# A feed-forward block sum in two passes, squares tile by tile, and single PSUM banks from the third pair of units on: one edit to a three-layer kernel

## The chip, the cores and the metric

The kernel runs on one core of a Trainium2 chip. The engines of that core are TensorE (PE), VectorE (DVE), ScalarE (ACT), GpSimd (POOL) and SyncE (SP, which here only issues transfers); data lie in SBUF (128 partitions) and matmul results in PSUM. The metric is the device time of one execution in microseconds (us), as a median over runs.

## The reference

Three residual layers over x of 1024 rows by 1024 columns, all fp32. Only the parts that the change touches, cut from the reference:

```python
fn = rms_norm(h, norm_ffn[l])
g = fn @ ffn_w_gate[l]                                  # 1024 x 2816
g_pad = jnp.pad(g, ((0, 0), (CONV_W - 1, 0), (0, 0)))
g_conv = ffn_conv_b[l] + sum(cw[i] * g_pad[:, i:i + s] for i in range(CONV_W))   # 3 taps
h = h + (jax.nn.silu(g_conv) * (fn @ ffn_w_up[l])) @ ffn_w_down[l]
...
return x + jnp.concatenate([y_a, y_b], axis=-1) @ w_out   # end of the second ("even") layer
```

Ahead of this stand a mixing stage (gated linear attention, "gla", and latent attention, "mla") and a cross attention ("xa"); behind it a state-space layer with a convolution branch ("even", whose end is `conf` in the code) and a differential attention ("odd"). Each adds a projection to the residual h, and rms_norm needs the row sums of squares of h.

## The kernel before, in words

**Numbers.** Every fp32 operand of a matmul is held as two parts, hi (rounded) and lo (the rest), and a product is three matmuls hi·hi, hi·lo, lo·hi (`mm3`, L258 to 265). `split` (L205) makes the parts of a PSUM tile: hi on ACT (L211), lo on VectorE (L212).

**Stages** in the profiled execution, in us from its start: gla and mla to about 640, xa to 759.5, the up projection of the feed-forward (`ffn_up`, L401) from 759.5 to 1226, the down projection (`ffn_down`, L492) to 1478, the even layer to 2187, its end `conf` to 2385, odd to 3091.

**Order.** The Tile framework plans each engine's queue ahead of time, from a priority that grows as the program is written, and from readiness. `later(n)` (L1261) shifts that priority by n for what is written inside it and sets it back at its end; AHEAD is 30. Each engine then works its queue in order. DMA transfers are issued from the queues of SP, of POOL and of ACT, and an issue stands in its engine's queue like any instruction.

**Memory.** `slot(tag)` takes the next buffer of a tagged set in turn; a buffer is free once its last readers are done. PSUM has four single banks of 512 columns (`pa`) and two pairs of banks of 1024 columns (`pb`), handed out by `psum` (L90).

**Residual tiles.** h is eight tiles of 128 x 1024. `load_h` (L94) takes eight buffers and loads tile t into the t-th: in gla (L834, from x), in the down projection (L507, issued from ACT's queue) and in conf (L1533, from `hs`). In conf, the third buffer of the eight lies on `zb`, from which ACT writes the SSD result to `ysp`; conf loads `ysp` back as `c` (L1525) behind the h loads, and casts it on ACT (L1527). `out_proj` (L295) multiplies and adds the result into h (`add_h`, L290); with `stats` it makes, after each fourth tile, the row statistics of four tiles (`row_stats`, L215: four Squares on ACT with a sum, L219, then the reciprocal root).

**Up projection.** The rows of h are two groups of four tiles, the columns two halves, so the product of 1024 x 1024 by 1024 x 256 is a 2 x 2 block product, done with seven block products in place of eight. There are 22 such units: 11 groups of 256 columns, each for the gate weight and then the up weight. A block product is 12 matmuls of 128 x 512 (`prod`). The weight blocks A11, A22, A12 and their sums S1 to S4 are made by `ffn_w` (L314): hi by ACT (L326), lo by VectorE or POOL (L327), sums by POOL (L332, L333, L334, L337). The input blocks B11, B21, B22 and sums T1 to T4 are made once, by `ffn_x` (L344), in two passes over the two row groups. Pass 0 (written inside `later(-AHEAD)`) scales rows, transposes (L359), splits B11 and B21 with `split`, and keeps a third, unrounded copy of each in `rows` (`xt`, ACT L382). Then `between` (L428) issues the two first products A11·B11 (`first`, L421, result copied to `p1`) and A12·B21 of units 0 and 1; the latter two stay in two single banks, `p2`, until their unit reads them. Pass 1 makes for each quarter k of the columns t1 (L387), t2 (L388), the split of B22, t3 and t4 on POOL (L390, L391), and hi and lo of T2, T3, T1 (lo on VectorE, L366) and T4 (lo on POOL, L366). Then the units run: S2·T2, A12·B21, S3·T3, S1·T1, A22·T4, S4·B22, each result added from PSUM by VectorE (`total` L454, `part` L448); a gate unit then does its three-tap convolution (L477, two taps for each of two blocks on VectorE), an up unit multiplies into it on POOL (L450) and stores the block to `yf` from SP's queue (L482). The pool `fg` (L1978) holds four `tmp` buffers for the sums.

**Down projection.** `yr` is loaded from `yf` on SP's queue (L501), cast on ACT (L503), and multiplied; the first transfer is behind the last stores in SP's queue.

## Time and profile before

| | us |
|---|---|
| median of 3 runs | 3098.76 |
| lowest and highest | 3096.89, 3098.79 |
| the profiled execution's own time | 3093.24 |
| its span, first to last instruction | 3091.2 |
| mean granted clock of TensorE in it | 0.980 of full |

Times in the profile are in us from the start of the span. Busy time of an engine is time in which it executes; what stands in brackets behind an instruction in a timeline is the time for which the engine sat idle before it, and what released it. `out<-in` names the tiles an instruction writes and reads. PEclk is the TensorE clock that was granted, as a share of full speed, which is 2.4 GHz; the lower of its two levels is 1.2 GHz.

### The profile page before, as it was taken

Reading aid. Unit: us, or ns where it says so; the run is one execution under the profiler, and the core shown is the slowest. Engines: PE = TensorE matmul, PEld = TensorE weight load, DVE = VectorE, ACT = ScalarE, POOL = GpSimd, SP = SyncE. Lnnn points to the kernel's source line nnn. Section 1 sums busy time; section 2 is a strip of 40 time slices with the busy share of each in tenths; the row PEclk is TensorE's granted clock in tenths of the full one; section 3 lists DMA queues with packets and bytes.
Section 4 is the critical chain, followed back from the end, with each engine's and each line's share of the span. In section 5 each row is a group of like instructions: output and inputs, shape, how many; then the busy total and the mean of one; then the engine's idle time right before and its main releaser. Section 6 shows DMA issues by size and latency. Waiting matters only on the chain.

```text
span 3091.2 us, 39184 instructions
## 1 busy us (share of the span) xinstructions
PE 2907.2 (94%) x14470; PEld 2364.7 (76%) x14470; DVE 2062.9 (67%) x3296; ACT 1196.4 (39%) x2264; POOL 1014.5 (33%) x917
## 2 busy tenths in 40 slices
PE   8999899898799999999998989999999999999998
PEld 7777676677588887788877878787777888878776
DVE  4225889865755555443798979787698454178786
ACT  5421666634433333221432322323234332155654
POOL 2112610122555554321125151524331231121444
PEclk9999999899899999999999999999999999999999
DMA  3012100212122223421311211122522446244531
GB/s 120 28 48 66 35 1 8 69 42 75 48 82 82 85 86 117 166 96 44 99 48 55 62 48 48 59 59 68 211 75 96 121 143 186 78 139 143 167 93 65
DMA packets 179380, 259.93 MB, mean 84 GB/s; under 512 B 16606, under 2 KB 107254, under 8 KB 179190
## 3 DMA queue, kind: packets, MB, share of 16 engines
q1 hardware_dynamic: 157813, 219.69, 22.4%
q10 hardware_dynamic: 16768, 20.98, 2.1%
q0 software_dynamic: 4608, 16.78, 1.4%
q8 instruction: 114, 1.87, 0.2%
q14 instruction: 77, 0.62, 0.1%
HBM read 191.33 MB, written 66.06 MB: 83 GB/s over the span
## 4 chain that ended last, share of the span: by engine, by line
PE 66%; DVE 15%; issue 5%; POOL 4%; ACT 3%; DMA 3%; SPq 0%; POOLq 0%; ACTq 0%; DVEq 0%
PE pa_t L263 16%; PE pa_t L264 16%; PE pa_t L265 15%; PE pb_t L265 3%; PE pb_t L264 3%; PE pb_t L263 3%; DVE acc_t L1311 3%; PE pa_t L941 2%; PE pb_t L1036 1%; PE pa_t L1055 1%; DVE wl_t L202 1%; PE pb_t L1750 1%; PE pb_t L1751 1%; ACT wh_t L197 1%; DVE h_t L292 1%
## 5 line engine op out<-in xcount | busy, mean ns | idle before, releaser
L202 POOL TENSOR_TENSOR wl_t<-wr_t,wh_t 128x349 fp32r<-128x349 f32 (+3 forms) x199 | 239.0, 1207 | 976.0 <-ACT wh_t L197 942.2
L263 PE MATMUL pa_t<-wh_t,x_t 128*128 128x512 f32 (+3 forms) x1024 | 374.3, 366 | 2.6 <-DVE xl_t L212 0.8
L264 PE MATMUL pa_t<-wl_t,x_t 128*128 128x512 f32 (+3 forms) x1024 | 371.3, 363 | 0.3 <-DVE wl_t L202 0.3
L1311 DVE SCALAR_TENSOR_TENSOR acc_t<-u_t,c,acc_t 128x1024 f32<-128x1024 f32 x240 | 339.4, 1416 | 2.9
L197 ACT CAST wh_t<-wr_t 128x1024 fp32r<-128x1024 f32 (+2 forms) x199 | 175.5, 890 | 354.2 <-PE pb_t L264 138.3
L290 DVE TENSOR_TENSOR h_t<-h_t,pa_t 128x512 f32<-128x512 f32 x256 | 173.1, 684 | 175.3 <-PE pa_t L265 171.8
L202 DVE TENSOR_TENSOR wl_t<-wr_t,wh_t 128x675 fp32r<-128x675 f32 (+2 forms) x173 | 170.9, 991 | 169.1 <-ACT wh_t L197 168.6
L263 PE MATMUL pb_t<-x_t,wh_t 128*128 128x512 f32 x608 | 244.3, 402 | 3.7 <-ACT wh_t L197 2.9
L265 PE MATMUL pb_t<-x_t,wl_t 128*128 128x512 f32 x608 | 242.2, 399 | 1.0 <-DVE wl_t L202 1.0
L264 PE MATMUL pb_t<-x_t,wh_t 128*128 128x512 f32 x576 | 231.0, 401 | 0.0
L265 PE MATMUL pa_t<-wh_t,x_t 128*128 128x512 f32 (+3 forms) x640 | 221.4, 346 | 0.0
L263 PEld LDWEIGHTS pa_t<-wh_t,x_t 128*128 128x128 f32 x1024 | 192.3, 188 | 33.6 <-ACT wh_t L197 1.8
L264 PEld LDWEIGHTS pa_t<-wl_t,x_t 128*128 128x128 f32 x1024 | 192.5, 188 | 30.9 <-DVE wl_t L202 2.0
L265 PE MATMUL pa_t<-wh_t,xl_t 128*128 128x512 f32 x512 | 200.4, 392 | 3.0 <-POOL xl_t L1848 2.1
L326 ACT CAST wh_t<-wr_t 128x512 fp32r<-128x512 f32 x154 | 92.1, 620 | 243.0 <-POOL wr_t L334 129.3
L263 PE MATMUL pa_t<-x_t,wh_t 128*128 128x512 f32 x400 | 163.9, 410 | 2.8 <-ACT xt_t L382 2.1
L265 PE MATMUL pa_t<-x_t,wl_t 128*128 128x512 f32 x400 | 158.8, 397 | 0.0
L327 DVE TENSOR_TENSOR wl_t<-wr_t,wh_t 128x512 fp32r<-128x512 f32 x110 | 97.7, 907 | 91.0 <-ACT wh_t L326 91.0
L263 PE MATMUL pa_t<-xh_t,wh_t 128*128 128x512 f32 x352 | 138.9, 395 | 5.3 <-DVE tmp_t L454 4.8
L263 PEld LDWEIGHTS pb_t<-x_t,wh_t 128*128 128x128 f32 x608 | 115.5, 190 | 30.8 <-ACT wh_t L197 3.9
L264 PE MATMUL pa_t<-xt_t,wh_t 128*128 128x512 f32 x352 | 138.2, 392 | 0.4 <-DVE xt_t L366 0.4
L265 PE MATMUL pa_t<-xh_t,wl_t 128*128 128x512 f32 x352 | 137.8, 392 | 0.0
(558 smaller groups left out, 7477.9 us busy)
## 6 DMA issues: line engine op xcount, KB each, us to landing
wr_t<-in_a_w_in SPq DMA_DIRECT2D x46, 512.0 KB
wr_t<-in_c_w_in SPq DMA_DIRECT2D x26, 512.0 KB
wr_t<-in_ffn_w_gate SPq DMA_DIRECT2D x22, 512.0 KB
wr_t<-in_ffn_w_up SPq DMA_DIRECT2D x22, 512.0 KB
yf<-o_t SPq DMA_DIRECT2D x22, 512.0 KB
wr_t<-in_ffn_w_down SPq DMA_DIRECT2D x44, 256.0 KB
yr_t<-yf SPq DMA_DIRECT2D x22, 512.0 KB
h_t<-in_x SPq DMA_DIRECT2D x16, 512.0 KB
```

Of the source, the lines that this page charges most:

```text
L197: nc.scalar.copy(hi, raw)
L202: e.tensor_tensor(*[x[:, c] for x in f], op=ALU.subtract)
L263: mm(out, lh, rh, start=st, stop=False)
L264: mm(out, lh, rl, start=False, stop=False)
L265: mm(out, ll, rh, start=False, stop=en)
L290: self.nc.vector.tensor_tensor(h[t][:, c], h[t][:, c], ps, op=ALU.add)
L292: self.nc.vector.scalar_tensor_tensor(h[t][:, c], ps, rstd[:, t:t + 1], h[t][:, c], op0=ALU.mult, op1=ALU.add)
L326: nc.scalar.copy(hi, src)
L327: eng.tensor_tensor(lo, src, hi.bitcast(F32), op=ALU.subtract)
L941: self.nc.tensor.transpose(pt[:, i * 256 + q * P:i * 256 + (q + 1) * P], w[t0 + q][:, (b0 + i) * P:(b0 + i + 1) * P], self.ident)
L1036: mm(sp[:, c0:c0 + wd], qT[:96, hd, t * P:(t + 1) * P], kT[:96, hd, c0:c0 + wd], start=True, stop=c0 + wd < n)
L1311: nc.vector.scalar_tensor_tensor(acc, u[:, k:k + S], cw31(k, c), acc, op0=ALU.mult, op1=ALU.add)
```

## The change

`load_h` takes its eight buffers rotated by half: tiles 0 to 3 lie in the last four, tiles 4 to 7 in the first four. `out_proj` with `stats` writes the Square of each tile right behind that tile's adds, and the reciprocal root behind the fourth. In pass 0 of `ffn_x`, B11 gets hi on ACT, its unrounded copy on VectorE from PSUM, and lo on POOL from that copy; B21 gets hi and the copy on ACT and lo on VectorE. `between` is called inside `later`, so that the priority is set back behind it. Pass 1 is split in two loops with the new `third` between them: the first makes t1, t2 (now in buffers of h that are no longer used), B22 and T2 with lo on POOL; `third` issues S4·B22 of units 0 and 1; the second makes t3 (now on VectorE), t4, and hi and lo of T3, T1, T4. A pair of banks of `pb`, halved by `two`, holds `p2` and the third product `p3` of each of units 0 and 1, and later S1·T1 and A22·T4 of unit 1; from the third unit on all products use single banks, as before. The last unit's two stores go out on POOL's queue, and `fg` has seven `tmp` buffers.

```diff
--- before.py
+++ after.py
@@ -93,6 +93,7 @@
 
     def load_h(self, src, eng=None):
         h = [self.slot("h", [P, D]) for _ in range(NT)]
+        h = h[NT // 2:] + h[:NT // 2]
         for t in range(NT):
             (eng or self.nc.sync).dma_start(out=h[t], in_=src[t * P:(t + 1) * P, :])
         return h
@@ -306,8 +307,13 @@
                     self.nc.gpsimd.tensor_tensor(h[t][:, c], h[t][:, c], d, op=ALU.add)
                 else:
                     self.add_h(h, t, c, ps, rstd)
-            if stats is not None and t % 4 == 3:
-                stats[t - 3] = self.row_stats(h[t - 3:t + 1])
+            if stats is not None:
+                if t % 4 == 0:
+                    self.ss = self.stat(4)
+                self.nc.scalar.activation(self.psum("pb"), h[t], AF.Square, accum_out=self.ss[:, t % 4:t % 4 + 1])
+                if t % 4 == 3:
+                    stats[t - 3] = self.stat(4)
+                    self.rsqrt(stats[t - 3], self.ss, D, EPS, 4, self.stat)
 
 
 
@@ -341,7 +347,7 @@
         return out
 
 
-    def ffn_x(self, h, st, hf, between):
+    def ffn_x(self, h, st, hf, between, third):
         nc = self.nc
         X = {n: [[x[:, i] for i in range(2)] for x in (self.slot(tag, [P, 2, 512], F32R) for _ in range(4))]
              for n, tag in (("B11", "x"), ("B21", "x"), ("B22", "xz"))}
@@ -373,28 +379,40 @@
                         nc.scalar.activation(t, t, AF.Copy, scale=st[g0][:, j:j + 1])
                     else:
                         v.tensor_scalar(t, t, st[g0][:, j:j + 1], None, op0=ALU.mult)
+                tt, g = [], nc.gpsimd
                 for k in range(4):
                     c1, c2 = self.col("norm_ffn", k), self.col("norm_ffn", k + 4)
                     p1, p2 = turn(g0, k), turn(g0, k + 4)
                     if i == 0:
-                        for n, p, c, r in (("B11", p1, c1, rows[k][0]), ("B21", p2, c2, rows[k][1])):
-                            self.split(*X[n][k], p, c)
-                            nc.scalar.activation(r, p, AF.Copy, scale=c)
+                        r1, r2 = rows[k]
+                        for (hi, lo), p, c, r in ((X["B11"][k], p1, c1, r1), (X["B21"][k], p2, c2, r2)):
+                            nc.scalar.activation(hi, p, AF.Copy, scale=c)
+                            if r is r1:
+                                v.tensor_scalar(r, p, c, None, op0=ALU.mult)
+                                g.tensor_tensor(lo, r, hi.bitcast(F32), op=ALU.subtract)
+                            else:
+                                v.scalar_tensor_tensor(lo, p, c, hi.bitcast(F32), op0=ALU.mult, op1=ALU.subtract)
+                                nc.scalar.activation(r, p, AF.Copy, scale=c)
                         continue
-                    ta, tb = (self.slot("wr", [P, 2, 512]) for _ in range(2))
-                    t1, t2, t3, t4 = ta[:, 0], ta[:, 1], tb[:, 0], tb[:, 1]
-                    b11, b21 = rows[k]
-                    v.scalar_tensor_tensor(t1, p1, c1, b11, op0=ALU.mult, op1=ALU.subtract)
+                    t12 = self.slot("h", [P, 2, 512])
+                    t1, t2 = t12[:, 0], t12[:, 1]
+                    v.scalar_tensor_tensor(t1, p1, c1, rows[k][0], op0=ALU.mult, op1=ALU.subtract)
                     v.scalar_tensor_tensor(t2, p2, c2, t1, op0=ALU.mult, op1=ALU.subtract)
                     self.split(*X["B22"][k], p2, c2)
-                    nc.gpsimd.tensor_tensor(t3, t2, b11, op=ALU.subtract)
-                    nc.gpsimd.tensor_tensor(t4, t2, b21, op=ALU.subtract)
-                    halves("T2", k, t2, v)
+                    halves("T2", k, t2, g)
+                    tt.append((t1, t2))
+                if i == 0:
+                    between(X)
+                    continue
+                third(X)
+                for k, (t1, t2) in enumerate(tt):
+                    t34 = self.slot("wr", [P, 2, 512])
+                    t3, t4 = t34[:, 0], t34[:, 1]
+                    v.tensor_tensor(t3, t2, rows[k][0], op=ALU.subtract)
+                    g.tensor_tensor(t4, t2, rows[k][1], op=ALU.subtract)
                     halves("T3", k, t3, v)
                     halves("T1", k, t1, v)
-                    halves("T4", k, t4, nc.gpsimd)
-            if i == 0:
-                between(X)
+                    halves("T4", k, t4, g)
         return X
 
 
@@ -412,8 +430,8 @@
                 self.wd = self.down_w(0)
 
 
-        def prod(w, x):
-            ps = self.psum()
+        def prod(w, x, ps=None):
+            ps = self.psum() if ps is None else ps
             for k in range(4):
                 self.mm3(ps, [(w[0][:, k], w[1][:, k])], [x[k]], k == 0, k == 3)
             return ps
@@ -429,10 +447,20 @@
             for i in range(2):
                 first(i, X)
             for i in range(2):
-                p2[i] = prod(ws[i]["A12"], X["B21"])
-
-        p2 = {}
-        X = self.ffn_x(h, st, hf, between)
+                p2[i], p3[i] = two()
+                prod(ws[i]["A12"], X["B21"], p2[i])
+
+        def third(X):
+            for i in range(2):
+                prod(ws[i]["S4"], X["B22"], p3[i])
+
+
+        def two():
+            ps = self.psum("pb")
+            return ps[:, 0:512], ps[:, 512:1024]
+
+        p2, p3 = {}, {}
+        X = self.ffn_x(h, st, hf, between, third)
         more()
         gt = {}
         for i, (kind, g) in enumerate(units):
@@ -462,11 +490,12 @@
             if i:
                 load(i + 1)
             u3 = total(u2, prod(w["S3"], X["T3"]))
-            p5 = prod(w["S1"], X["T1"])
+            p5, p4 = two() if i == 1 else (None, None)
+            p5 = prod(w["S1"], X["T1"], p5)
             part(1, hb, u3, p5)
             u4 = total(u2, p5)
-            part(1, ha, u3, prod(w["A22"], X["T4"]), ALU.subtract)
-            part(0, hb, u4, prod(w["S4"], X["B22"]))
+            part(1, ha, u3, prod(w["A22"], X["T4"], p4), ALU.subtract)
+            part(0, hb, u4, p3[i] if i < 2 else prod(w["S4"], X["B22"]))
             if gate:
                 gt[g] = []
                 for j in (0, 1):
@@ -479,7 +508,7 @@
                     gt[g].append(o)
             else:
                 for j in (1, 0):
-                    nc.sync.dma_start(out=yf[2 * g + j], in_=O[j])
+                    (nc.gpsimd if i == len(units) - 1 else nc.sync).dma_start(out=yf[2 * g + j], in_=O[j])
 
 
     def down_w(self, f0):
@@ -1975,7 +2004,7 @@
                 with K.pool("xf", x=8, xh=16, xt=16, xz=4), ExitStack() as fs:
                     def more():
                         hctx.close()
-                        fs.enter_context(K.open(K.pool("fg", o=2, tmp=4, g=2)))
+                        fs.enter_context(K.open(K.pool("fg", o=2, tmp=7, g=2)))
                     K.ffn_up(h, st, hf, yf, cw, more)
                 hctx = K.open(K.pool("h1b", "right", h=8))
                 with K.pool("fd", yr=2, ya=8, yb=8):
```

## Rows read from the trace of the kernel before

**Rows 1.** The page: busy time, share of the span and instructions of each engine.
```profile
PE 2907.2 (94%) x14470; PEld 2364.7 (76%) x14470; DVE 2062.9 (67%) x3296; ACT 1196.4 (39%) x2264; POOL 1014.5 (33%) x917
```

**Rows 2.** Stretches: length, busy PE, PEld, DVE, ACT, POOL (instructions), clock, DMA share, GB/s.
```profile
761.00:778.00 17.00, 4.66 (x20) 2.98 (x20) 13.09 (x26) 11.40 (x22) 8.37 (x7) 0.66 0.43 137
778.00:792.00 14.00, 13.85 (x52) 11.26 (x53) 5.96 (x8) 8.35 (x15) 6.43 (x5) 0.81 0.05 18
792.00:816.00 24.00, 13.27 (x55) 9.30 (x53) 22.20 (x25) 12.09 (x21) 16.32 (x13) 0.72 0.08 23
...
830.00:845.00 15.00, 9.95 (x36) 7.81 (x37) 13.33 (x14) 7.82 (x9) 7.18 (x6) 0.89 0.23 71
845.00:1214.00 369.00, 369.00 (x1629) 305.66 (x1628) 215.01 (x271) 131.27 (x195) 206.50 (x156) 1.00 0.25 83
1226.00:1247.00 21.00, 13.51 (x43) 9.02 (x43) 3.88 (x4) 4.80 (x5) 6.84 (x5) 0.84 0.92 329
2190.00:2215.00 25.00, 21.15 (x90) 16.26 (x89) 14.29 (x28) 5.87 (x7) 1.93 (x2) 1.00 0.87 335
2215.00:2255.00 40.00, 36.22 (x157) 28.75 (x156) 40.00 (x42) 14.13 (x14) 26.44 (x9) 1.00 0.44 169
```

**Rows 3.** Waits of PE, 760 to 830: total us, times, longest.
```profile
PE pa_t L359 <- DVE wr_t L387: 10.0, 4, 4.5
PE pa_t L359 <- ACT xt_t L382: 9.0, 3, 6.0
```

**Rows 4.** Timeline of PE, 838 to 846: start, us, instruction, idle before and releaser.
```profile
838.07 0.80 PE L263 MATMUL pa_t<-xh_t,wh_t 128*128 128x512 f32 x1 [4.76 <-DVE tmp_t L454]
...
845.22 0.39 PE L263 MATMUL pa_t<-x_t,wh_t 128*128 128x512 f32 x1
```

**Rows 5.** Timeline of DVE, 829 to 846.
```profile
831.54 5.87 DVE L477 SCALAR_TENSOR_TENSOR o_t<-g_t,c,o_t 128x1023 f32<-128x1023 f32 x4
```

**Rows 6.** Lines 366 and 387, 755 to 830: duration in ns min/median/max, starts.
```profile
L366 DVE TENSOR_TENSOR xt_t<-wr_t,xh_t x12: 678/1722/1783, 795.3 to 816.0; 128x512 fp32r<-128x512 f32 x12
...
L366 POOL TENSOR_TENSOR xt_t<-wr_t,xh_t x4: 1540/1550/1581, 797.2 to 815.6; 128x512 fp32r<-128x512 f32 x4
...
L387 DVE SCALAR_TENSOR_TENSOR wr_t<-pa_t,c,xt_t x4: 734/743/751, 792.3 to 806.0; 128x512 f32<-128x512 f32 x4
```

**Rows 7.** Timelines of ACT and of POOL in the first pass.
```profile
772.10 2.18 ACT L326 CAST wh_t<-wr_t 128x512 fp32r<-128x512 f32 x4 [3.75 <-POOL wr_t L334]
774.18 0.68 ACT L382 ACTIVATE xt_t<-pa_t,c 128x512 f32<-128x512 f32 x1
...
770.80 1.26 POOL L334 TENSOR_TENSOR wr_t<-wr_t 128x512 f32<-128x512 f32 x1
```

**Rows 8.** Timeline of ACT at the end of the down projection.
```profile
1461.66 1.03 ACT L219 ACTIVATE pb_t<-h_t 128x1024 f32<-128x1024 f32 x1 [1.57 <-DVE h_t L290]
```

**Rows 9.** Timelines of SP and of PE at the start of the down projection.
```profile
1226.46 0.42 SPq L501 DMA_DIRECT2D yr_t<-yf  x1
1228.80 0.32 SPq L482 DMA_DIRECT2D yf<-o_t  x1
1229.16 0.43 SPq L501 DMA_DIRECT2D yr_t<-yf  x1
...
1232.00 0.79 PE L263 MATMUL pa_t<-wh_t,ya_t 128*128 128x512 f32 x1 [5.82 <-ACT ya_t L503]
```

**Rows 10.** Start of conf: SP's timeline, SP's waits, and what line 1527 waited for.
```profile
2197.13 3.37 SPq L97 DMA_DIRECT2D h_t<-hs  x6
...
SPq L97 <- DMA ysp<-zb_t: 7.0, 1, 7.0
...
  DMA c_t<-ysp: 15.8, 2
```

**Rows 11.** The last h load of gla on SP, and tile 3's add on DVE.
```profile
264.81 0.33 SPq L97 DMA_DIRECT2D h_t<-in_x  x1
...
272.19 0.69 DVE L290 TENSOR_TENSOR h_t<-h_t,pa_t 128x512 f32<-128x512 f32 x1 [2.15 <-PE pa_t L265]
```

## The prediction

> **What bounds the kernel now.** I read the busy times of the page first: TensorE is busy for 2907.2 of 3091.2 us, 94% [rows 1], so an edit pays only where TensorE waits, or crawls at its lower clock, inside the stretches that the diff touches. A table by stretch comes next [rows 2]. From 845 to 1214 us, the steady part of the up projection, TensorE is busy for all 369.00 us at clock 1.00: 1629 matmuls, 0.2265 us each, and nothing that frees another engine is worth anything there. The waste lies in five places. At the entry (761 to 778) TensorE is busy for 4.66 of 17 us at 0.66 of full clock; in the second pass (792 to 816) for 13.27 of 24 at 0.72; in the first pair of units (830 to 845) for 9.95 of 15 at 0.89; where the up projection hands over to the down projection (1226 to 1247) for 13.51 of 21 at 0.84; at the start of conf (2190 to 2215) for 21.15 of 25. The last three views say who is late. TensorE's waits between 760 and 830 name the scaled copy `xt` made on ACT (9.0 us, first pass) and VectorE's subtraction L387 (10.0 us in four waits, second pass) [rows 3]. The timeline shows one more stop, 4.76 us up to 838.07, released by VectorE's `total` L454 [rows 4]: VectorE had spent 5.87 us from 831.54 on four conv taps [rows 5] while the four single banks, one of them held by unit 1's `p2`, stood full with nobody to read them. Unit 2 begins at 845.22 [rows 4].
>
> **The change, part by part.** *Second pass and the first two units.* Between 792 and 845.2 TensorE does ten products of 12 matmuls (five each for units 0 and 1). At 0.2265 us, 120 matmuls are 27.2 us of the 53.2; the other 26 are 32 transposes, waiting and half clock. Before, each of the four steps k puts on VectorE, in order, L387, L388, the low part of B22, and three subtractions of L366 (T2, T3, T1), and the transposes of the next step wait for a bank that VectorE reads only after those. L387 takes 0.74 us and reads PSUM; L366, with both inputs in SBUF, takes 0.678 us at the least but 1.72 us in the median [rows 6]. POOL works beside it: 1.55 us for each of its own four of L366 [rows 6], and I give its eight of t3 and t4 the 1.26 us of L334, of the same shape [rows 7]. 1.72 is 0.68 and most of such an operation, so I read this as the two engines taking turns. By that reading the section is 12 x 0.68 + 8 x 1.26 + 4 x 1.55 = 24.4 us, and it measures 25 (L387 first at 792.3, VectorE's L366 last at 816.0).
>
> After the change the first loop holds only operations that read PSUM on VectorE: 12 x 0.743 = 8.9 us, with POOL's four low parts of T2 (5.0 us) beside them, so with the first start near 792.3 and a little for the transposes all of B22 and T2 is done near 802; before, L387, the first operation of a step, came last at 806.0 [rows 6]. TensorE then has 36 matmuls ready (the third product S4·B22 of units 0 and 1, and S2·T2 of unit 0), 8.2 us, that need nothing from the second loop. That loop costs 12 x 0.68 on VectorE (t3, low T3, low T1) and 8 x 1.26 on POOL (t4, low T4): 18.2 us in turns, so it ends near 820.2. What is left for TensorE then is the last quarter of A22·T4 and the four products of unit 1, 51 matmuls or 11.6 us, so 831.8. I add 1.7 us for a restart at the lower level, as after the stop, when 24 matmuls took the 7.15 us from 838.07 to 845.22 and not 5.44: 833.5 against 845.2, **12 us gained**. The stop at 838 goes: with the pairs of `pb`, the four products of unit 1 have a bank each, 10.9 us of work, more than the 5.87 us of taps; seven `tmp` slots are part of this and are worth nothing on their own. The lower bound is 5.4 us (24 matmuls moved under the pass, all else as it is), the upper 22 (of the 26, some 4 remain, an estimate for 32 transposes at half a matmul each).
>
> The Trainium skill, "SBUF — State Buffer", section "SBUF: two separate sides", says that a VectorE instruction with two SBUF inputs and a GpSimd instruction that reads SBUF lock each other out of a shared port pair, and that the loser stops. This trace agrees (0.678 alone, 1.72 beside POOL). It speaks against the second loop, which keeps 12 such instructions beside 8 of POOL; without it that loop would be 10.1 us, TensorE would never wait in it, and the gain would be 15 in place of 12.
>
> *First pass.* Each k loses one of ACT's two copies `xt` (L382, 0.68 us [rows 7]) and gets a VectorE scaling from PSUM in its place; the low part of B11 moves from VectorE to POOL, four operations at 1.26. TensorE waited 9.0 us for ACT's copies [rows 3], but ACT itself stood 3.75 us up to 772.10 for POOL's chain s1, s3, s2 that ends with L334 at 770.80 plus 1.26 [rows 7]. What is put ahead of that chain on POOL's queue comes out at 772.10 later. ACT sheds 4 x 0.68 = 2.7 us; POOL gains 5.0. Bounds: 5 lost (all four ahead of the chain) to 5 gained (half of the 9.0, its part behind no POOL wait). POOL is busy for 8.37 of the 17 us [rows 2], so some have room before the chain: **1 gained**.
>
> *Between the passes* TensorE is busy 13.85 of 14 us [rows 2]; that `between` now shares a place with the second pass changes nothing there by itself, as TensorE has no slack to reorder into.
>
> *Squares tile by tile.* They are that already: the second square of the down projection starts at 1461.66, 1.57 us after the one before, released by its own tile's add L290 [rows 8]. **0.** If the old order had hidden them at group ends, the cost would be up to four of 1.03 us at a group's end; it doesn't.
>
> *The last two stores on POOL's queue.* On SP, the load of `yr` 0 goes out at 1226.46 behind the first store; the second store waits for POOL's product until 1228.80 and the load of `yr` 1 stands behind it till 1229.16. TensorE restarts at 1232.00 after 5.82 us, released by the ACT cast of `yr` 0 [rows 9]. Moving the stores lets `yr` 0 go by the 0.32 us of a store's issue sooner, and `yr` 1 by up to 2.7 (1229.16 less 1226.46). But DMA is at 0.92 of its time from 1226 to 1247 [rows 2], and the later casts are paced by it. Bounds 0.3 to 5.8 (the whole stop); **2**, since the early issue reaches the wire partly.
>
> The Trainium skill, "DMA: Bandwidth & Descriptors", section "Issuing engines are not separate DMA queues", says that issuing from several engines saves only the sequencer's time. The row shows more than that, a load standing behind a store that waits for POOL; by the rule alone the gain would be about 0.3.
>
> *`load_h` rotated.* In conf, SP waits 7.0 us at L97 for the write ysp<-zb and then, at 2197.13, issues six of the eight loads in 3.37 us; the load c<-ysp, for which ACT L1527 waits 15.8 us, goes out behind them [rows 10]. The third handle is the slot that `zb` held. Rotated, it is the seventh tile's, so four more loads go out before the wait and c<-ysp 4 x 0.56 = 2.2 us sooner, with 2 MB fewer ahead of it (6.3 us at the 335 GB/s of the stretch). TensorE idles 3.85 us in 2190 to 2215, and VectorE has 40.00 of 40 us to do after it [rows 2], so what comes sooner is worth its time only up to the idle. Bounds: 3.9 gained; 3 lost, if the 6.3 us of early loads delay the write of ysp by what doesn't fit into the free 13% of 25 us. **3 gained.** In gla the last load goes out at 264.81 and becomes tile 3's, whose add runs at 272.19 after TensorE [rows 11], 7.4 us later: **0**, at most the 2.15 us wait of that add.
>
> **Sum.** 12 + 1 + 2 + 3 = 18. The profiled execution took 3093.24 us (span 3091.2), so 3075.2; the median of the runs, 3098.76, is 5.5 higher, so 3080.8, call it 3081.
>
> **Rivals.** *T blocks too late.* If the second loop is late enough that TensorE, after its 36 matmuls, falls to its lower level for a good part of the 51 that follow (at 1.2 for 2.4 GHz, 20 of them cost 20 x 0.2265 = 4.5 us more), the gain of the second pass is 6 to 8 and the time 3085 to 3087. For it: 18.2 us of loop against 8.2 of cover. Against: T3 and T1 come block by block and are used so. *Nearly all waste gone.* Engines side by side, 15, and 4 at the hand-over, 4 and 4 elsewhere: 3068 to 3072. For it: stretches at 0.66 to 0.72 of clock lift themselves once filled. *No net effect.* The planner of the queues puts the third products behind the second loop, so only banks change: gain 5.4 or less, with the bounds of the other parts: 3092 to 3100. *Slower.* In the first pass POOL's queue holds all four new low parts ahead of the chain to L334. Each of them waits for its step's transposes, and these wait for banks that ACT empties, while ACT stands before the copies of S2 that wait for L334: its stop grows from 3.75 us by the 5.0 and a step or two of the pass (17 us for four), to 12 or more. Unit 1's chain can do it once more. Two such stops lose some 20 us; the other gains (17) are eaten up, and as POOL then also brings T2 late, most of the 12 doesn't come: 3105 to 3110. It decides from a loss of 12 us there on if the second pass gains nothing, from 24 if it gains all. For it: ACT's wait for L334 is there today. Against: one weight chain alone lies in the 17 us, and the order on POOL follows when inputs are ready.
>
> **How the numbers follow.** The runs differ by 2 us; 0.2%, 6.2 us, is about what can be told from no change. Forecast (3073 to 3084) 0.52; T blocks late (3084 to 3092) 0.22; nearly all gone (3062 to 3073) 0.12; none (3092 to 3105) 0.09; slower 0.05. Faster 0.86, same 0.09, slower 0.05. A range from 3065 to 3092 leaves out the slower two and a little of the best.
>
> **What the profile after would show.** Right: no wait of TensorE for L387 over 2 us; matmuls of S4·B22 directly behind the last transposes; unit 2 starting 12 us sooner after the entry; no stop behind the taps; `yr` 1 issued within 0.5 us of `yr` 0; only two h loads of conf behind ysp<-zb. Wrong: `between`'s products pushed behind the second pass; ACT waiting over 5 us for L334; the conf loads delaying the ysp write; a steady part (369 us) with holes because three banks of four are too few.

## The result, and the profile after

The changed kernel takes 3086.02 us (median of 5 runs, 3080.09 to 3087.35) against 3098.76 before (5 runs, 3096.89 to 3107.0): ratio 0.995, interval 0.9935 to 0.9965. That is 12.7 us faster where 17.8 were forecast (3081); the range, 3065 to 3092, holds it. The profiled execution took 3087.35 us, with a span of 3085.2.

The table by stretch is read first, now of the kernel after. The first five stretches answer to the entry, the time between the passes, the second pass, the first pair of units and the steady part of [rows 2], moved by the 3.8 us by which this execution reaches the entry later; the last two are the hand-over and the start of conf.

```profile
764.80:781.80 17.00, 10.11 (x35) 7.14 (x36) 13.77 (x25) 10.25 (x19) 11.56 (x9) 0.70 0.37 121
781.80:795.80 14.00, 9.92 (x53) 7.15 (x52) 10.04 (x13) 7.87 (x14) 11.70 (x9) 1.00 0.12 37
795.80:819.80 24.00, 17.68 (x65) 11.73 (x64) 21.40 (x23) 11.26 (x20) 18.15 (x12) 0.89 0.15 44
833.80:848.80 15.00, 15.00 (x68) 12.30 (x67) 8.29 (x12) 6.43 (x9) 12.47 (x9) 1.00 0.24 70
848.80:1206.00 357.20, 356.85 (x1575) 295.26 (x1574) 213.28 (x269) 128.88 (x193) 202.48 (x153) 1.00 0.27 86
1217.40:1238.40 21.00, 13.23 (x48) 9.02 (x47) 5.44 (x6) 5.48 (x6) 8.87 (x7) 0.92 0.93 333
2182.20:2207.20 25.00, 21.16 (x90) 16.26 (x89) 14.25 (x28) 5.96 (x7) 1.72 (x2) 1.00 0.89 338
```

TensorE is busy 10.11 of 17 us at the entry (before 4.66), 17.68 of 24 in the second pass (13.27) at clock 0.89 (0.72), and the first pair of units fills its 15 us. Between the passes it is busy for less, 9.92 of 14 (13.85), but with as many matmuls, 53 (52), as the clock is 1.00 there and was 0.81: busy time counts for more work at the higher clock, so the number of matmuls is the better measure. The steady part stays full. Conf is as it was: 21.16 of 25, before 21.15.

TensorE's waits between 764 and 834, the longest four:

```profile
PE pa_t L265 <- DVE xt_t L372: 4.3, 4, 1.6
PE pa_t L365 <- ACT xt_t L395: 3.0, 2, 2.1
PE pb_t L264 <- ACT wh_t L332: 1.6, 1, 1.6
PE pa_t L365 <- DVE h_t L399: 1.4, 1, 1.4
```

The waits of 10.0 us for VectorE's t1 and of 9.0 for ACT's copy [rows 3] are down to 1.4 (L399 is the new number of L387) and 3.0. What is new on top is a wait of 4.3 us for VectorE's low parts (L372), in four pieces. Which part of the change took the two old waits away, the run with the pairs of banks alone shows below.

**A ruler for the feed-forward part.** The stretch from the last issue of `hf` on POOL to the start of the last matmul of the up projection leaves out whatever happens ahead and behind. Timelines of the kernel before:

```profile
760.55 0.53 POOL L353 DMA_DIRECT2D hf<-h_t  x1 [4.91 <-DVE h_t L290]
...
1225.80 0.39 PE L265 MATMUL pa_t<-xz_t,wl_t 128*128 128x512 f32 x1
```

and of the kernel after:

```profile
764.31 0.53 POOL L359 DMA_DIRECT2D hf<-h_t  x1 [4.91 <-DVE h_t L291]
...
1218.32 0.39 PE L266 MATMUL pa_t<-xz_t,wl_t 128*128 128x512 f32 x1
```

465.24 us before, 454.01 after (from unrounded times): **11.2 us** gained. The first row also shows the 3.8 us lost ahead of it, where the experiments show that nothing was changed. Four executions of code that is unchanged in this stretch give 464.99 to 466.31, so a figure of this ruler is good to about 1 us. The time of a kernel moves by several us from run to run.

**Where it is gained.** In every trace the ruler holds the same number of matmuls, 1902, the transposes among them. So the number of matmuls done some time after the last `hf` issue tells how far TensorE has come, at 0.2265 us for each in the steady part [rows 2]. At about 55 us the second pass ends, and by 85 us the stop behind VectorE's conv taps is over. The kernel before, then the kernel after:

```profile
760.55:815.55 55.00, 31.75 (x127) 23.31 (x125) 40.80 (x57) 32.28 (x55) 31.21 (x24) 0.72 0.18 58
760.55:845.55 85.00, 56.60 (x226) 43.12 (x225) 61.90 (x81) 43.02 (x69) 45.90 (x35) 0.80 0.20 62
```

```profile
764.31:819.31 55.00, 37.65 (x150) 25.84 (x149) 44.83 (x58) 29.87 (x52) 41.89 (x29) 0.86 0.21 65
764.31:849.31 85.00, 67.65 (x278) 50.43 (x277) 63.78 (x83) 41.90 (x69) 60.04 (x43) 0.90 0.20 62
```

The lead is 23 matmuls (5.2 us) at 55 us and 52 (11.8 us) at 85 us. So less than half of the gain arises in the two passes, and the rest behind them, where the stop of 4.76 us was. In the four executions of unchanged code these counts are 126 to 128 and 221 to 227.

**The hand-over.** Timelines of SP, POOL and TensorE after the change, against [rows 9]:

```profile
1217.88 0.90 SPq L530 DMA_DIRECT2D yr_t<-yf  x2
...
1221.57 0.59 POOL L511 DMA_DIRECT2D yf<-o_t  x1 [0.30 <-POOL o_t L478]
...
1223.63 0.51 PE L264 MATMUL pa_t<-wh_t,ya_t 128*128 128x512 f32 x1 [4.92 <-ACT ya_t L532]
```

Both loads of `yr` go out within 0.9 us, ahead of the last store, and the stop is 4.92 us in place of 5.82. Against the last matmul of the up projection the first load goes out 1.1 us sooner than before, the second 3.3 us.

**Conf.** SP's waits and its timeline after the change, against [rows 10]:

```profile
SPq L98 <- DMA ysp<-zb_t: 7.1, 1, 7.1
...
2189.40 2.97 SPq L98 DMA_DIRECT2D h_t<-hs  x6
```

Nothing has changed: the wait is 7.1 us (7.0), and six loads still stand behind it. The prediction had two there.

### The profile page after: what moved, and what is told of

It reads as the page before. It is cut to its first block, busy times and chain, and to the rows that moved or that the text cites. A ratio compares the mean times of both kernels' runs of the same rounds, so it can differ in the third digit from the quotient of the medians.

```text
span 3085.2 us, 39147 instructions
## 1 busy us (share of the span) xinstructions
PE 2910.8 (94%) x14462; PEld 2364.3 (77%) x14470; DVE 2059.0 (67%) x3296; ACT 1192.9 (39%) x2260; POOL 1028.5 (33%) x923
## 4 chain that ended last, share of the span: by engine, by line
PE 64%; DVE 16%; issue 5%; POOL 4%; DMA 4%; ACT 3%; SPq 0%; POOLq 0%; DVEq 0%; ACTq 0%
PE pa_t L264 15%; PE pa_t L265 15%; PE pa_t L266 15%; DVE acc_t L1340 4%; PE pb_t L266 3%; PE pb_t L265 3%; PE pb_t L264 3%; PE pa_t L970 2%; PE pb_t L1065 1%; PE pa_t L1084 1%; DVE wl_t L203 1%; PE pb_t L1779 1%; PE pb_t L1780 1%; POOL wl_t L203 1%; DVE h_t L293 1%
## 5 line engine op out<-in xcount | busy, mean ns | idle before, releaser
L264 PE MATMUL pb_t<-x_t,wh_t 128*128 128x512 f32 x616 | 247.9, 402 | 4.4 <-ACT wh_t L198 1.9
L265 PE MATMUL pb_t<-x_t,wh_t 128*128 128x512 f32 x584 | 233.7, 400 | 0.3 <-DVE x_t L394 0.3
L266 PEld LDWEIGHTS pb_t<-x_t,wl_t 128*128 128x128 f32 x616 | 116.7, 189 | 30.1 <-DVE wl_t L203 3.5
L209 ACT CAST pt_t<-pa_t 128x512 fp32r<-128x512 f32 (+2 forms) x240 | 104.8, 443 | 81.9 <-PE pa_t L970 46.0
```

The source lines that it names most:

```text
L209: nc.scalar.copy(hi, src)
L264: mm(out, lh, rh, start=st, stop=False)
L265: mm(out, lh, rl, start=False, stop=False)
L266: mm(out, ll, rh, start=False, stop=en)
```

## The experiments

The column "stretch" is the ruler above, and the last column has the matmuls done 24, 55 and 85 us after the last `hf` issue. The time of each kernel is compared with runs of the kernel before on the same chip (medians 3095.85, 3097.08 and 3094.69 in the three groups).

| kernel | median us | ratio to before, interval | stretch | gained in it | matmuls at 24, 55, 85 us |
|---|---|---|---|---|---|
| before | | | 465.24 | | 41, 127, 226 |
| after | 3086.02 | 0.995, 0.9935 to 0.9965 | 454.01 | 11.2 | 65, 150, 278 |
| rotation alone | 3099.37 | 1.0011, 1.0002 to 1.002 | 464.99 | 0.2 | 42, 127, 227 |
| Squares alone | 3095.73 | 1.0, 0.9991 to 1.0009 | 466.31 | -1.1 | 43, 128, 221 |
| feed-forward part alone | 3084.01 | 0.9972, 0.996 to 0.9984 | 453.59 | 11.7 | 65, 151, 279 |
| stores alone | 3095.5 | 1.0003, 0.9992 to 1.0014 | 465.45 | -0.2 | 41, 126, 225 |
| pairs of banks alone | 3091.83 | 0.9979, 0.997 to 0.9989 | 460.39 | 4.9 | 59, 146, 247 |
| after, no early third | 3090.43 | 0.9975, 0.9964 to 0.9987 | 460.19 | 5.1 | 66, 146, 248 |
| after, engines of before | 3081.92 | 0.9953, 0.9937 to 0.997 | 454.65 | 10.6 | 65, 153, 278 |
| after, second loop on VectorE | 3083.03 | 0.9951, 0.9935 to 0.9968 | 449.99 | 15.3 | 65, 184, 294 |
| after, first pass as before | 3089.03 | 0.9978, 0.9969 to 0.9987 | 457.14 | 8.1 | 45, 149, 262 |
| after, `between` outside | 3082.11 | 0.9959, 0.9946 to 0.9972 | 452.34 | 12.9 | 60, 165, 292 |
| second loop on VectorE, single banks | 3085.19 | 0.9966, 0.9953 to 0.9979 | 450.95 | 14.3 | 65, 183, 297 |
| that, and low B11 on VectorE | 3077.28 | 0.9945, 0.993 to 0.9959 | 448.32 | 16.9 | 43, 187, 306 |

**Rotation alone.**

```diff
         h = [self.slot("h", [P, D]) for _ in range(NT)]
+        h = h[NT // 2:] + h[:NT // 2]
```

> The kernel before with only the rotated buffers of load_h. Theory 1 (the feed-forward input alone carries the change; the rotation gives nothing and costs a little): no difference that can be told, within 4 us of before; in the trace gla about 1 us later by 300 us, as in the changed kernel, and conf not sooner than before against the end of the stage ahead of it, because what conf waits for is the write of ysp and not the h loads. Theory 2 (my prediction's term): 3 us faster, all of it between 2185 and 2220 us, with c<-ysp issued some 2.2 us sooner after the wait for ysp<-zb.

Built, this kernel consists of the same instructions as the one before, on each engine in the same order, with the same addresses. So the framework gives a buffer its address in the order of use, and not when `slot` is called. Tile 2 of conf lies on `zb` as it did. So neither theory holds: there is no edit to measure, and this run shows what chance makes of one program, 3.5 us of median and an interval that does not hold 1.

**Squares alone.**

```diff
-            if stats is not None and t % 4 == 3:
-                stats[t - 3] = self.row_stats(h[t - 3:t + 1])
+            if stats is not None:
+                ...
+                self.nc.scalar.activation(self.psum("pb"), h[t], AF.Square, accum_out=self.ss[:, t % 4:t % 4 + 1])
```

> The kernel before with only the Squares written tile by tile. Theory 1 (the planned order of ACT shifts around them at the end of mla and in xa): 1 to 2.5 us slower by 760 us in the trace, with the shift arising between 555 and 690 us, as the changed kernel showed (3.8 us late at 760, of which some 1.3 before 400). Theory 2 (the prediction: the Squares ran tile by tile already, so nothing moves): 0 within 0.5 us at every mark, and the 3.8 us belong to the rotation or to chance of the run.

The same again: the built program is that of before, as the planner had placed the Squares by readiness already. Theory 2 holds in its reason, but not at its marks: the trace comes to 760 us 3.7 us later than that of before, with the same program. The lag of the kernel after at that place is thus no effect of the change.

**Feed-forward part alone.** The diff without `load_h`, `out_proj` and the two stores.

> The kernel before with the whole edit of the feed-forward input and of the units (two loops, third product between, pairs of banks, between inside later, seven tmp buffers), without rotation, Squares and stores. Theory 1 (this part is the whole gain): 11 us gained between 760 and 900 us of the trace, time 10 to 15 us below before, as fast as the changed kernel or 2 to 4 us faster, since nothing is lost ahead of 760 us. Theory 2 (a third of the gain lies in the hand-over and conf): 8 us below before or less.

11.7 us in the stretch, 11.8 between the medians. Theory 1 holds. The interval of the ratio (1.6 to 4 parts in 1000 below 1) and that of the kernel after (3.5 to 6.5) overlap little; after what the first two runs show of one program that is no sign of a difference, and the stretch, 453.59 against 454.01, puts the two kernels level.

**Stores alone.**

```diff
-                    nc.sync.dma_start(out=yf[2 * g + j], in_=O[j])
+                    (nc.gpsimd if i == len(units) - 1 else nc.sync).dma_start(out=yf[2 * g + j], in_=O[j])
```

> The kernel before with only the last unit's two stores on POOL's queue. Theory 1 (early issue of the load of yr 1 is worth about 1 us, as DMA is nearly full there): 0.5 to 1.5 us sooner by 1260 us, time within 3 us of before. Theory 2 (my prediction's term): 2 us sooner by 1260 us, with TensorE's stop of 5.82 us down to 4 or less.

The stop at the hand-over is 4.96 us. From the last matmul of the up projection to the first of the down projection the five kernels with the stores on SP take 6.13 to 6.34 us (mean 6.23), the nine with them on POOL 4.40 to 6.46 (mean 5.38): some 0.85 us. Theory 1 fits; in the time it can't be seen.

**Pairs of banks alone.** Before, with p2 of units 0 and 1 in pairs, their S4·B22 at its old place in the other half, and a pair for unit 1's S1·T1 and A22·T4.

```diff
-                p2[i] = prod(ws[i]["A12"], X["B21"])
+                p2[i], p3[i] = two()
+                prod(ws[i]["A12"], X["B21"], p2[i])
...
-            p5 = prod(w["S1"], X["T1"])
+            p5, p4 = two() if i == 1 else (None, None)
+            p5 = prod(w["S1"], X["T1"], p5)
```

> The kernel before with the pairs of banks alone: p2 of units 0 and 1 in pairs, unit 1's S1·T1 and A22·T4 in one more pair, unit 0's and 1's S4·B22 in the other halves at its old place. The measure is the lead over before that the trace gains between the marks at 740 and 1000 us (the whole edit gained 11.5). Theory 1 (the prediction: banks take away the stop of 4.76 us at 838 and its restart, and let the transposes run ahead): 4 to 7 us. Rival (banks alone were the limit of the second pass, as TensorE waited there for banks that VectorE had not read): 9 us or more.

4.9 us: the size is theory 1's, the place only half of it. 19 matmuls of the lead (4.3 us) are there at 55 us and only 21 at 85 us:

```profile
761.94:816.94 55.00, 35.84 (x146) 25.15 (x144) 42.17 (x58) 32.76 (x56) 32.71 (x25) 0.84 0.18 58
761.94:846.94 85.00, 60.92 (x247) 45.12 (x246) 64.08 (x81) 42.99 (x69) 50.43 (x37) 0.88 0.20 62
```

The transposes do run ahead. TensorE's two old waits [rows 3] are down with the pairs alone (762 to 847 us):

```profile
PE pa_t L359 <- DVE wr_t L387: 5.2, 2, 4.6
PE pa_t L359 <- ACT xt_t L382: 3.0, 2, 1.8
```

The stop of 4.76 us [rows 4], however, doesn't go. It splits into two of 2.48 and 1.71, as S4·B22 now waits for the reading of its pair's first half.

**No early third.** The line `third(X)` is taken out, and S4·B22 of units 0 and 1 goes to the end of the unit, into `p3`.

> The changed kernel with S4·B22 of units 0 and 1 at its old place at the end of the unit, all else kept. Theory 1 (the 24 matmuls cover the second loop): 3 to 5.4 us of the 11.5 lost. Rival (the planner interleaves other products as well, so that cover is not short): less than 1.5 lost.

5.1 us are left of 11.2 to 11.7, so 6.2 to 6.6 lost, more than theory 1's 3 to 5.4. TensorE's timeline shows two stops that the kernel after does not have:

```profile
812.28 0.80 PE L265 MATMUL pa_t<-xt_t,wh_t 128*128 128x512 f32 x1 [4.31 <-POOL xt_t L372]
...
842.46 0.80 PE L264 MATMUL pb_t<-xz_t,wh_t 128*128 128x512 f32 x1 [4.43 <-DVE tmp_t L475]
```

The first is missing cover, with POOL's low parts not ready; the second is S4·B22 of unit 1, behind VectorE's taps. The counts tell the two apart:

```profile
769.88:824.88 55.00, 36.52 (x146) 25.28 (x145) 47.35 (x60) 29.64 (x52) 42.24 (x29) 0.84 0.22 69
769.88:854.88 85.00, 62.09 (x248) 45.94 (x247) 66.41 (x82) 41.12 (x68) 60.72 (x43) 0.86 0.20 62
```

At 55 us this kernel is 4 matmuls (0.9 us) behind the kernel after (150), at 85 us it is 30 behind (278). So the reason of theory 1, cover for the second loop, is worth about 0.9 us by this count. Most of the loss lies behind the taps, where the two products come back to the end of their units.

**Engines of before.**

```diff
-                    halves("T2", k, t2, g)
+                    halves("T2", k, t2, v)
...
-                    v.tensor_tensor(t3, t2, rows[k][0], op=ALU.subtract)
+                    g.tensor_tensor(t3, t2, rows[k][0], op=ALU.subtract)
```

> The changed kernel with the engines of before for two operations: low T2 on VectorE, t3 on POOL; loops, third and pairs kept. Theory 1 (VectorE's operations with two SBUF inputs and POOL's take turns, so that only their sum counts, but low T2 on VectorE holds up the reading of PSUM in the first loop): 1 to 4 us of the 11.5 lost. Rival (which engine does it is of no account, as the count of operations of both is the same): within 0.7.

10.6 us, 0.6 to 1.1 less: within what chance does to this stretch, so the rival (within 0.7) can't be told from the low end of theory 1. Which engine does which of these eight operations matters little while both work side by side.

**Second loop on VectorE.**

```diff
-                    g.tensor_tensor(t4, t2, rows[k][1], op=ALU.subtract)
+                    v.tensor_tensor(t4, t2, rows[k][1], op=ALU.subtract)
...
-                    halves("T4", k, t4, g)
+                    halves("T4", k, t4, v)
```

> The changed kernel with the second loop wholly on VectorE: t4 and low T4 too, POOL does none of it. Theory 1 (taking turns: 12 x 0.68 + 8 x 1.26 = 18.2 us in turns against 20 x 0.68 = 13.6 on one engine): the operations of the loop take 0.68 us and not 1.76, it ends about 4 us sooner, and 1 to 4 us more are gained by 1000 us. Rival (side by side but for chance, or POOL's work on weights takes the same turns): no gain, or 2 to 3 us lost because VectorE does 8 operations more.

15.3 us, 3.6 to 4.0 more than with POOL's help. Lines 372 and 411 on VectorE (duration in ns, min/median/max, and starts) in the kernel after:

```profile
L372 DVE TENSOR_TENSOR xt_t<-wr_t,xh_t x4: 694/1760/1765, 805.0 to 816.5; 128x512 fp32r<-128x512 f32 x4
...
L372 DVE TENSOR_TENSOR xt_t<-h_t,xh_t x4: 679/1222/1762, 805.6 to 818.2; 128x512 fp32r<-128x512 f32 x4
...
L411 DVE TENSOR_TENSOR wr_t<-h_t,xt_t x4: 676/1216/1769, 789.1 to 811.4; 128x512 f32<-128x512 f32 x4
```

and in this run:

```profile
L372 DVE TENSOR_TENSOR xt_t<-wr_t,xh_t x8: 677/680/682, 802.7 to 812.8; 128x512 fp32r<-128x512 f32 x8
...
L411 DVE TENSOR_TENSOR wr_t<-h_t,xt_t x4: 680/681/1291, 786.7 to 808.6; 128x512 f32<-128x512 f32 x4
...
L412 DVE TENSOR_TENSOR wr_t<-h_t,xt_t x4: 678/680/1783, 798.4 to 811.0; 128x512 f32<-128x512 f32 x4
```

POOL's timeline in this run shows it idle for most of the loop:

```profile
815.59 1.49 POOL L333 TENSOR_TENSOR wl_t<-wr_t,wh_t 128x512 fp32r<-128x512 f32 x1 [11.05 <-ACT wh_t L332]
```

The same operations take 0.68 us while POOL is silent, against 1.76 in the median of T3's low parts beside POOL. Eight operations more on one engine end sooner than with two (813.5 us, 51.5 after the last `hf` issue, against 54.6): theory 1.

**First pass as before.** In pass 0, `self.split(*X[n][k], p, c)` and ACT's copy for both blocks.

> The changed kernel with the first pass as before: B11 and B21 split by ACT and VectorE, both unrounded copies on ACT, nothing on POOL. The measure is again the lead over before that is gained between the marks at 740 and 1000 us (the whole edit: 11.3 and 11.7). Theory 1 (the prediction's term: ACT's copies cost more than POOL's new low parts): about 1 us less, 10 to 10.7. Rival (POOL's four low parts delay the weight sums s1, s3, s2, for which ACT now waits 18 us in all): 1 to 3 us more, 12.3 or above.

8.1 us, 3.1 to 3.6 less than with the edit: the rival falls, and theory 1's 10 to 10.7 is missed too. The place is not the first pass, as two stretches and a stop in TensorE's timeline show:

```profile
766.28:821.28 55.00, 36.38 (x149) 25.71 (x148) 42.08 (x57) 32.25 (x56) 34.70 (x25) 0.84 0.21 66
766.28:851.28 85.00, 63.89 (x262) 47.93 (x261) 63.00 (x84) 44.72 (x74) 53.52 (x39) 0.88 0.20 62
...
842.68 0.50 PE L264 MATMUL pb_t<-xh_t,wh_t 128*128 128x512 f32 x1 [2.49 <-DVE tmp_t L476]
```

At 24 us this kernel has done 45 matmuls against 65, but at 55 us the two are level (149 and 150): the second pass uses up the head start. The loss of 16 matmuls (3.6 us) comes after it, with a stop of 2.49 us behind the taps that the kernel after does not have. Why VectorE reads that bank later here was not followed up. In the first pass POOL's new low parts, 5.0 us of work, delay the chain of weight sums by about 1.5 us: ACT's four casts that wait for the chain start 13.3 us after the last `hf` issue in the kernel after and 11.7 us after it here. In the kernel after, then here:

```profile
777.58 2.18 ACT L332 CAST wh_t<-wr_t 128x512 fp32r<-128x512 f32 x4 [4.27 <-POOL wr_t L340]
```

```profile
778.01 2.18 ACT L332 CAST wh_t<-wr_t 128x512 fp32r<-128x512 f32 x4 [3.30 <-POOL wr_t L340]
```

**`between` outside.** The call goes back behind the `with` block.

> The changed kernel with the four first products written outside the shifted priority, as before. Theory 1 (the prediction: their place in the order is worth nothing by itself): 10.5 to 12.5 us of lead. Rival (inside it the planner mixes them with the transposes of the second pass, which the trace of the changed kernel shows, and the mixing is a part of the gain): 6 to 9.5 us.

12.9 us, 1.3 to 1.7 more than inside: a little beyond theory 1's upper bound and about at the limit of the ruler. Its new place gains nothing.

**Second loop on VectorE, single banks.** As the run with the loop on VectorE, with p5 and p4 of unit 1 from `psum()`.

> The second loop wholly on VectorE, as in the run that gained 15.3 us, and unit 1's S1·T1 and A22·T4 in single banks in place of one pair. Theory 1 (the stop of 2.70 us at 832.8 in that run is A22·T4 waiting until VectorE, behind the conv taps, has read its pair's other half): the stop goes, 16 to 18 us of lead. Rival (single banks are then short for the next unit): a stop of the same length one product later, 14.5 to 15.5.

14.3 us. TensorE's timelines around the stop, in the run with the pair and in this one:

```profile
832.78 0.80 PE L264 MATMUL pb_t<-xh_t,wh_t 128*128 128x512 f32 x1 [2.70 <-DVE tmp_t L482]
```

```profile
832.97 0.47 PE L264 MATMUL pa_t<-xh_t,wh_t 128*128 128x512 f32 x1 [2.33 <-DVE tmp_t L482]
```

The stop stays. The rival holds, though 14.3 lies 0.2 below its range: in the order of the built program the product that waits is no longer A22·T4 of unit 1 but S2·T2 of unit 2. TensorE has caught up with VectorE's conv taps, and some bank has to wait for them.

**And low B11 on VectorE.** On top of that run:

```diff
-                                g.tensor_tensor(lo, r, hi.bitcast(F32), op=ALU.subtract)
+                                v.scalar_tensor_tensor(lo, p, c, hi.bitcast(F32), op0=ALU.mult, op1=ALU.subtract)
```

> As the one with the second loop on VectorE and single banks, and the low part of B11 in the first pass made by VectorE from PSUM and not by POOL. Theory 1 (POOL's low parts hold up the weight sums, and VectorE's reading from PSUM shares no turn with POOL): 0.5 to 2.5 us more than that one. Rival (VectorE is the later engine in the first pass): 0.5 to 2 us less.

16.9 us, 2.6 more: the size is theory 1's, a little above its range, but its reason is not shown. In the first 24 us this kernel has done 43 matmuls and the run before 65, and TensorE waits for VectorE's low part of B11, as the rival has it:

```profile
PE pa_t L264 <- DVE x_t L392: 2.8, 1, 2.8
```

At 55 us it leads by 4 (187 and 183). Most of its gain comes later, with a stop behind the taps of 0.77 us in place of 2.33:

```profile
826.03 0.47 PE L264 MATMUL pa_t<-xh_t,wh_t 128*128 128x512 f32 x1 [0.77 <-DVE tmp_t L482]
```

The second pass is full in this run, where the kernel after was at 17.68 of 24. That is the work of the loop on VectorE, as it is nearly full in the run before too. The run before, then this one:

```profile
794.29:818.29 24.00, 23.42 (x97) 17.40 (x97) 24.00 (x35) 11.71 (x21) 8.10 (x6) 0.96 0.21 67
```

```profile
790.00:815.00 25.00, 24.29 (x107) 18.93 (x106) 23.52 (x36) 11.70 (x22) 10.47 (x8) 1.00 0.20 64
```

With 3077.28 us it is the fastest kernel of the study, 17.4 below the median of before on its chip. Its interval overlaps that of the kernel after; the stretch, 5.7 us shorter, tells the two apart.

## Why the prediction was right, and where not

The direction, the stage and the range were right, and the forecast of 18 us was 5 too large: about 3 in conf, 1.1 at the hand-over, and 1.3 to 1.8 in the feed-forward input. The median, 3086.02, lies among the times that the prediction gave to its rival "T blocks too late" (3084 to 3092) and not among those of its forecast (3073 to 3084). The rival's waits are there (4.3 us for low parts), but not its small gain (6 to 8); with the missing 3 us of conf the time would lie in the forecast's range. By its terms:

**Second pass and first pass, 12 and 1.** Together 13 were forecast and 11.2 to 11.7 measured. The sum is near, but the way to it was not as described, and that is in part luck.

The step that failed is "TensorE then has 36 matmuls ready" for the second loop. The planner did not put both third products behind the last transposes. It mixed unit 0's with them, all but one matmul between 791.2 and 806.1 us, and unit 1's came only at 826.17, when the second loop had ended (818.9). These rows of TensorE's timeline show it:

```profile
791.21 0.40 PE L264 MATMUL pb_t<-xz_t,wh_t 128*128 128x512 f32 x1
...
795.07 1.09 PE L365 MATMUL pa_t<-c,h_t 128*128 128x128 f32 x8 [1.13 <-DVE xz_t L213]
795.92 0.47 PE L265 MATMUL pb_t<-xz_t,wh_t 128*128 128x512 f32 x1
...
826.17 0.39 PE L264 MATMUL pb_t<-xz_t,wh_t 128*128 128x512 f32 x1
...
834.33 0.39 PE L264 MATMUL pa_t<-x_t,wh_t 128*128 128x512 f32 x1
```

So the third products hardly covered the second loop, and TensorE waited 4.3 us for low parts. Against that the second pass began sooner than the forecast took it to, which kept the 792.3 of before, 31.8 us after the last `hf` issue. VectorE's L399 (before L387) starts 20.6 us after it:

```profile
L399 DVE SCALAR_TENSOR_TENSOR h_t<-pa_t,c,xt_t x4: 735/739/743, 784.9 to 799.0; 128x512 f32<-128x512 f32 x4
```

The two errors about cancel. Unit 2 begins at 834.33, 70.0 us after the last `hf` issue and not 84.7 (845.22 less 760.55), with one product of unit 1 (2.7 us) still behind it: some 12 us sooner, as forecast.

The lead at the end of the two passes, 5.2 us at 55 us, comes mostly from the pairs, which by themselves bring 4.3 there as the transposes run ahead. The prediction gave the pairs the stop alone.

**The stop at 838.** It went as forecast, and is the larger part of the gain. It takes both the pairs and the third product done early: the pairs alone leave stops of 2.48 and 1.71 us, and without the early third product there is one of 4.43 us.

**First pass alone.** The term of 1 is neither shown nor refuted: leaving that edit out costs 3.1 to 3.6 us, but behind the taps. The wait of 9.0 us for ACT's copies went down to 3.0 with the pairs alone. ACT's longest wait for the weight sums is 5.5 us before and after, so that sign of being wrong ("over 5 us") told nothing.

**Taking turns.** The reading that VectorE's operations with two SBUF inputs and POOL's operations exclude each other, on which the 18.2 us of the second loop rested, is shown by the run with the loop on VectorE: 0.68 us against 1.76 for the same operation. The Trainium skill, "SBUF — State Buffer", section "SBUF: two separate sides", has this as a lock between the two engines, and these rows agree. In the kernel after, the loop ended at 818.9 (the last L372, 818.2 and 0.68), 54.6 us after the last `hf` issue, where the forecast's 820.2 lay 59.7 us after it: sooner, as the pass began sooner and some of the loop's operations (L411 from 789.1 on) were mixed into the first loop. The lock spoke against this change as the prediction said, and leaving POOL out gave 3.6 to 4.0 us more.

**Squares and gla: 0.** Right, and for a simpler reason than was given for gla: these edits leave the program as it was.

**Conf, 3.** Nothing came of it. The step that failed is "Rotated, it is the seventh tile's". The addresses follow the order of use, so that the tile that lay on `zb` still does. The gain from issuing those loads before the wait was not tried.

**Hand-over, 2.** The mechanism is right (both loads go out early, and the stop shrinks). The size is 0.9 in the profile shown and some 0.85 on average, though the loads go out 1.1 and 3.3 us sooner. DMA is at 0.93 of its time there (0.92 before), which fits a gain of a part only; that it is the reason was not tested. The Trainium skill, "DMA: Bandwidth & Descriptors", section "Issuing engines are not separate DMA queues", would have it at the issue time alone; the measured value lies above the 0.3 worked out from that, and well below the 2.

The sum by measured terms, 11.2 to 11.7 and 0.9, is 12.1 to 12.6, against 12.7 between the medians, which by themselves can't be told to better than some us.

## What to carry to other kernels

Before an edit of order or of buffers is priced, ask whether the planner keeps it: where it places by readiness and gives addresses in the order of use, a rotated list or a rewritten loop can be the same program. When VectorE and POOL share elementwise work on SBUF, compare the sum of both in turns with VectorE alone; 20 operations of 0.68 us beat 12 of them beside 8 of POOL. Measure small edits over the stretch that they touch: its chance here was about 1 us where the time of the same program moved by 3.5. And where a part is left out, look at which time the loss arises: leaving out the edit of the first pass, or the early third product, cost most of its time in a later stop, behind the taps.

## What the runs showed of the hardware that was not expected

In the fourteen traces the last `hf` issue lies between 758.85 and 769.88 us, though no kernel differs from the one before ahead of it. In the latest of them, that without the early third, some 5 of the 9.3 us of lag arise between 200 and 250 us, around the h loads of gla; the cause was not followed up. In the seam between the up and the down projection unchanged code moves by 0.2 us only (6.13 to 6.34).
